# First SwiGLU products: four plain pairs, four pairs by seven products, three plain pairs

## The chip, the core and the metric

The kernel runs on one core of one Trainium2 chip. TensorE (PE) multiplies matrices: a weight load (PEld) puts a 128x128 block into the array, and a matmul streams up to 512 columns past it and adds up in one of eight PSUM banks. VectorE (DVE) and ScalarE (ACT) work elementwise, GpSimd (POOL) does small things and issues transfers, and SyncE (SP) issues most transfers from HBM. The metric is device time in microseconds (us), the median of several runs.

## The reference

Two layers, each a half-step SwiGLU, a mixer and a second half-step SwiGLU, on x of 512 positions by 1024 features in float32; each step adds its result to x and normalizes. The part that matters here is the SwiGLU, which runs four times:

```python
def swiglu(x, w13, w2):
    a, b = jnp.split(x @ w13, 2, axis=-1)
    return (jax.nn.silu(a) * b) @ w2
...
    x = layer_norm(ALPHA * x + 0.5 * swiglu(x, ffn1_w13[l], ffn1_w2[l]), ln_g[l, 0], ln_b[l, 0])
```

`w13` is 1024 x 5632 (2816 for a, 2816 for b), `w2` is 2816 x 1024. "First products" are x @ w13, "second products" the ones with w2.

## The kernel before

Every float32 factor is split into a high part hi (rounded to the matmul type float32r, by ACT) and a rest lo (source minus hi, by DVE); `split` does both. A product is three matmuls: hi by hi, hi by lo, lo by hi.

**First products.** The 2816 hidden features are 22 blocks of 128. For block j, `blocks` fetches 128 columns of w13 for a and 128 for b (`weights`: a transfer of 512 KB into a `raw` tile, then the split into two `w` tiles), and takes two PSUM banks. `pair_of` multiplies them with x (`xh`, `xl`, features on partitions, 512 positions as columns): 8 steps over the 1024 features, 3 matmuls each, for a and for b. `glu` applies Silu on ACT (tile `sa`) and multiplies on DVE into the result tile r of pair k = j % 11: blocks k and k + 11 form a pair. In three of the four SwiGLUs the first two blocks run in halves of 256 positions, since x comes out of the normalization bit by bit (`need`), and their weights lie in other tiles (`early`).

**Second products.** The class `Seven` forms r @ w2 by Strassen's scheme in Winograd's form: per block pair, seven products of half-size blocks in place of eight, whose factors are sums and differences of quarters. `activation_sums(k)` makes the sums of r (DVE, split, and for k of 8 and more a copy to DRAM); `weight_sums(k)` loads 1 MB of w2, makes four sums on DVE and writes them to DRAM through POOL. Both follow each finished pair in `glu`. `run` then goes through the products in order of k, with `mm`, 3 matmuls of 512 columns at a time.

**Order.** The kernel is written for a layer that makes the engines' programs from this text: it sets all waits and gives out tiles by tag, and its queues need not follow the text's order. The tags that matter: `w` (10 tiles of 4 KB per partition, hi and lo of weights in work), `raw` (4, weights as loaded), `h` (33, everything that stays longer: x, r, sums, early weights), `rs` (2, w2 quarters while their sums are made), `sa` (3, half-size work tiles), `ps` (the 8 banks).

Of the kernel before, what the change touches and what calls it, by code (L numbers as in the profile page):

```python
# [24 lines left out]
F32 = mybir.dt.float32  # L28
F32R = mybir.dt.float32r
I32 = mybir.dt.int32  # L30
AF = mybir.ActivationFunctionType
ALU = mybir.AluOpType
AX = mybir.AxisListType

P = 128
D = 1024
T = 512
DEPTH = 2
DFF = 2816
NF = DFF // P  # L40
# [42 lines left out]
def trunk(ctx: ExitStack, tc, x_in, xt_in, w13, w2, w_in, w_br, w_out, ln_g, ln_b, lb_in, hgn, sgg, sgb, sgws,  # L83
          sgbs, masks, tril_in, ident_in, out):
    nc = tc.nc
    V, S, G, PE = nc.vector, nc.scalar, nc.gpsimd, nc.tensor
# [3 lines left out]
    wk = ctx.enter_context(tc.tile_pool(name="wk", bufs=1))  # L90
    psum = ctx.enter_context(tc.tile_pool(name="psum", bufs=8, space=bass.MemoryType.PSUM))

    flow = Flow()
    MM = 216.0

    def bank(name):
        return psum.tile([P, 512], F32, tag="ps", name=name)
# [4 lines left out]
    def slot(name, dtype=F32):  # L102
        return big.tile([P, 2, 512], dtype, tag="h", name=name, bufs=NS)
# [10 lines left out]
    xh, xl = [None] * 4, [None] * 4  # L114


    def split(hi, lo, src):
        S.activation(hi, src, AF.Copy)  # L118
        V.tensor_tensor(lo, src, hi.bitcast(F32), op=ALU.subtract)  # L119

    def weights(src, name, early=False):

        raw = wk.tile([P, D], F32, tag="raw", name=f"r_{name}", bufs=NRAW)
        nc.sync.dma_start(raw, src)
        if early:
            hi, lo = (slot(f"{c}_{name}", F32R).rearrange("p a t -> p (a t)") for c in "hl")
        else:
            hi, lo = (wk.tile([P, D], F32R, tag="w", name=f"{c}_{name}", bufs=NW) for c in "hl")
        split(hi, lo, raw)
        return hi, lo  # L130

    NW = 10
    NS, NRAW, NSA = 33, 4, 3

    def proj(ps, w, c0, mov, nk=KT, n0=0, n=T):

        hi, lo = w
        i = 0
        for k in range(nk):
            cs = slice(c0 + k * P, c0 + (k + 1) * P)  # L140
            mh, ml = mov(k)
            for a, m in ((hi, mh), (hi, ml), (lo, mh)):
                PE.matmul(ps[:, n0:n0 + n], a[:, cs], m[:, n0:n0 + n], start=(i == 0), stop=(i == 3 * nk - 1))  # L143
                i += 1
            flow.tick(3 * MM * n / T)
# [5 lines left out]
    def begin_features():  # L151
        for q in range(4):
            xh[q], xl[q] = slot(f"xh{q}", F32R), slot(f"xl{q}", F32R)
# [26 lines left out]
    H = slice(0, 512), slice(512, 1024)  # L180
# [6 lines left out]
    def norm(t, xt, sums, g, b, last, wait=11500.0):  # L187


        nm = small("nm")  # L190
        V.tensor_scalar(nm, sums[:, 0:1], sums[:, 1:2], -1.0 / D, op0=ALU.add, op1=ALU.mult)
        sq = wk.tile([P, D], F32, tag="rs", name="sq", bufs=2)
        ssq = small("ssq")
        S.activation(sq, xt, AF.Square, bias=nm, accum_out=ssq)
        rstd = rstd_of(ssq, 1, 1.0 / D, LN_EPS / ALPHA ** 2, "rstd")
        for qs in H:
            V.scalar_tensor_tensor(xt[:, qs], xt[:, qs], nm, g[:, qs], op0=ALU.add, op1=ALU.mult)
            V.scalar_tensor_tensor(xt[:, qs], xt[:, qs], rstd, b[:, qs], op0=ALU.mult, op1=ALU.add)
            if last:
                nc.sync.dma_start(out[0, t * P:(t + 1) * P, qs], xt[:, qs])  # L200
        if not last:
            x_at[t] = dram.tile([P, D], F32, name=f"xd{t}", tag=f"xd{t}", bufs=2)
            nc.gpsimd.dma_start(x_at[t], xt)
            ready[t] = flow.add(to_features(t, xt), wait)
# [3 lines left out]
    def need(*ts):  # L208
        for t in ts:
            if ready[t] is not None:  # L210
                flow.finish(ready[t])
                ready[t] = None
# [40 lines left out]
    def quads(name, dtype=F32):  # L253
        return slot(name, dtype).rearrange("p a t -> p (a t)").rearrange("p (q t) -> p q t", q=4)

    NH2 = NF // 2

    class Seven:
# [11 lines left out]

        def part(self, k, a):

            if k not in self.r:
                self.r[k] = quads(f"r{k}")
            return self.r[k][:, a::2, :]

        def weight_sums(self, k):
            w = self.w_of(k)
# [51 lines left out]
        def run(self, c, ln, last):  # L330
# [103 lines left out]
            for tt in range(2):  # L434
# [5 lines left out]
                add_to(xs[t], 0, c, F[tt], sums[t])  # L440
                norm(t, xs[t], sums[t], g, b, last)

    def ffn(l, i, last=False, first_of_all=False):
        made = list(range(Seven.KEPT, NH2)) + list(range(Seven.KEPT))
        seven = Seven(lambda k: w2[l, i, k])
        js = [j for k in made for j in (k, k + NH2)]

        def blocks(j, early=False):
            return (weights(w13[l, i, j], f"a{j}", early), weights(w13[l, i, NF + j], f"b{j}", early),
                    bank(f"pa{j}"), bank(f"pb{j}"))  # L450

        def pair_of(j, args, n0, n):
            wa, wb, pa, pb = args
            proj(pa, wa, 0, from_x, KT, n0, n)
            proj(pb, wb, 0, from_x, KT, n0, n)

        def glu(j, args):
            wa, wb, pa, pb = args
            k, a = j % NH2, j // NH2
            sa = wk.tile([P, T], F32, tag="sa", name="sa", bufs=NSA)  # L460
            S.activation(sa, pa, AF.Silu)
            V.tensor_tensor(seven.part(k, a), sa.rearrange("p (h t) -> p h t", h=2),  # L462
                            pb.rearrange("p (h t) -> p h t", h=2), op=ALU.mult)
            if a:
                seven.activation_sums(k)
                seven.weight_sums(k)

        start = 0 if first_of_all else 2
        first = [blocks(j, True) for j in js[:start]]
        need(0, 1)  # L470
        for z, j in enumerate(js[:start]):
            pair_of(j, first[z], 0, 256)
        need(2, 3)
        for z, j in enumerate(js[:start]):
            pair_of(j, first[z], 256, 256)
            glu(j, first[z])
        for z, j in enumerate(js[start:]):
            if z == 0 and first_of_all:
                begin_features()
                wa = load_wx(w13[l, i, j])  # L480
                for q in range(1, 4):
                    load_xt(q)
                wb = weights(w13[l, i, NF + j], "b0")
                args = wa, wb, bank("pa0"), bank("pb0")
            else:
                args = blocks(j)
            pair_of(j, args, 0, T)
            glu(j, args)
        seven.run(0.5 / ALPHA, (l, 2 * i), last)

    def gates():
# [353 lines left out]
    def load_xt(q):  # L845

        raw = wk.tile([P, D], F32, tag="raw", name=f"xt{q}", bufs=NRAW)
        nc.sync.dma_start(raw, xt_in[q])
        for k in range(2):
            split(xh[q][:, k, :], xl[q][:, k, :], raw[:, k * T:(k + 1) * T])  # L850

    def load_wx(w):

        raw = wk.tile([P, D], F32, tag="raw", name="r_a0", bufs=NRAW)
        hi, lo = (wk.tile([P, D], F32R, tag="w", name=f"{c}_a0", bufs=NW) for c in "hl")
        rx = wk.tile([P, D], F32, tag="raw", name="xt0", bufs=NRAW)
        for z in range(2):
            zs = slice(z * 512, (z + 1) * 512)
            nc.sync.dma_start(raw[:, zs], w[:, zs])
            nc.sync.dma_start(rx[:, zs], xt_in[0, :, zs])  # L860
            split(hi[:, zs], lo[:, zs], raw[:, zs])
            split(xh[0][:, z, :], xl[0][:, z, :], rx[:, zs])
        return hi, lo

    prep = flow.add(prepare(), 30000.0)
    for l in range(DEPTH):
        ffn(l, 0, first_of_all=(l == 0))
        if l == 0:
            flow.finish(prep)
        mixer(l, lb, om)  # L870
        ffn(l, 1, last=(l == DEPTH - 1))
# [98 lines left out]
```

## Time and profile before

| what | us |
| --- | --- |
| median of 3 runs | 2115.67 |
| range of these | 2115.6 to 2118.93 |
| profiled execution, its own time | 2116.28 |
| its span, first to last instruction | 2114.5 |
| first products of the first SwiGLU, first matmul | 5.7 |
| first Silu to last Silu over all four SwiGLUs | 16.4 to 1995.2 |

In the profile a line names the engine, the line of the kernel, the operation, the tile written and the tiles read, the shapes, a count, and then busy time and the mean duration of one in ns; the last field is the time that the engine sat idle before such instructions and what ended it. Timeline rows begin with start and duration in us. Tiles here: `pa`, `pb` the banks of a block, `h_a`, `l_a`, `h_b`, `l_b` its split weights, `r_a`, `r_b` these as loaded, `sa` the Silu, `ra_w`, `rb_w` the quarters of w2.

### The profile page before, as it was taken

The numbers are of one execution on the slowest core, as the hardware profiler recorded it, in microseconds if no ns is written. First come the engines' busy times: TensorE is split into PE (matmuls) and PEld (weight loads), VectorE is DVE, ScalarE is ACT, GpSimd is POOL, SyncE is SP. The second block draws the span as 40 slices with busy tenths as digits, with TensorE's granted clock in tenths as the row PEclk, the third lists the DMA queues.
The fourth block names the chain that finished last, engine by engine and source line by source line (L and its number), as shares of the span: only waits on it lengthen the run. The fifth ranks groups of instructions, "written<-read, shape, count | busy, mean of one in ns | idle before, by whom it ended". The sixth has DMA issues, their size and how long they took to land. (4 is left out here: it accounts for less than half of the span.)

```text
span 2114.5 us, 26531 instructions
## 1 busy us (share of the span) xinstructions
PE 2096.8 (99%) x10024; PEld 1760.8 (83%) x10024; DVE 1226.2 (58%) x2019; ACT 771.4 (36%) x1090; POOL 211.4 (10%) x360
## 2 busy tenths in 40 slices
PE   8999999999999999999999999999999999999998
PEld 6888888888888988888898888888888889888886
DVE  5545578853535745548754456779444456454586
ACT  4222354223422422225522224552343224222363
POOL 0101102001000211101111010020010001110101
PEclk9999999999999999999999999999999999999999
DMA  7665777122242465567756566761222425555674
GB/s 267 216 211 177 247 262 256 44 77 89 81 156 93 176 235 177 195 210 268 248 192 233 178 208 234 270 230 41 90 81 91 143 95 208 205 200 198 223 258 146
DMA packets 113904, 381.01 MB, mean 180 GB/s; under 512 B 14320, under 2 KB 14576, under 8 KB 113776
## 3 DMA queue, kind: packets, MB, share of 16 engines
q1 hardware_dynamic: 88848, 291.68, 42.1%
q0 software_dynamic: 24928, 87.64, 10.9%
q8 instruction: 78, 1.28, 0.3%
q14 instruction: 50, 0.41, 0.1%
HBM read 311.11 MB, written 68.16 MB: 179 GB/s over the span
## 5 line engine op out<-in xcount | busy, mean ns | idle before, releaser
L143 PE MATMUL pa<-xh,h_a 128*128 128x512 f32 (+1 forms) x752 | 284.4, 378 | 6.2 <-ACT xh L118 6.1
L143 PE MATMUL pa<-xl,h_a 128*128 128x512 f32 (+1 forms) x752 | 284.5, 378 | 0.0
L143 PE MATMUL pa<-xh,l_a 128*128 128x512 f32 (+1 forms) x752 | 283.6, 377 | 0.0
L143 PE MATMUL pb<-xh,h_b 128*128 128x512 f32 (+1 forms) x752 | 282.8, 376 | 0.0
L143 PE MATMUL pb<-xh,l_b 128*128 128x512 f32 (+1 forms) x752 | 282.4, 375 | 0.0
L143 PE MATMUL pb<-xl,h_b 128*128 128x512 f32 (+1 forms) x752 | 282.3, 375 | 0.0
L119 DVE TENSOR_TENSOR l_b<-r_b,h_b 128x1024 fp32r<-128x1024 f32 x132 | 161.6, 1225 | 166.8 <-ACT h_b L118 166.3
L118 ACT ACTIVATE h_b<-r_b 128x1024 fp32r<-128x1024 f32 x132 | 140.0, 1061 | 303.6 <-PE pa L143 245.8
L462 DVE TENSOR_TENSOR r<-sa,pb 128x512 f32<-128x512 f32 x88 | 60.6, 688 | 302.0 <-PE pb L143 302.0
L118 ACT ACTIVATE h_a<-r_a 128x1024 fp32r<-128x1024 f32 (+1 forms) x89 | 93.5, 1051 | 274.3 <-PE pb L143 264.7
L143 PEld LDWEIGHTS pa<-xh,h_a 128*128 128x128 f32 x752 | 142.1, 189 | 33.1 <-ACT xh L118 7.4
L143 PEld LDWEIGHTS pa<-xl,h_a 128*128 128x128 f32 x752 | 142.2, 189 | 27.8 <-DVE xl L119 2.0
L143 PEld LDWEIGHTS pa<-xh,l_a 128*128 128x128 f32 x752 | 142.2, 189 | 25.4
L143 PEld LDWEIGHTS pb<-xh,h_b 128*128 128x128 f32 x752 | 141.5, 188 | 25.7
L143 PEld LDWEIGHTS pb<-xl,h_b 128*128 128x128 f32 x752 | 141.5, 188 | 25.6
L143 PEld LDWEIGHTS pb<-xh,l_b 128*128 128x128 f32 x752 | 141.4, 188 | 25.5
L119 DVE TENSOR_TENSOR l_a<-r_a,h_a 128x1024 fp32r<-128x1024 f32 (+1 forms) x89 | 107.8, 1211 | 11.2 <-ACT h_a L118 7.3
L143 PE MATMUL z<-xh,h_z 128*128 128x512 f32 x256 | 102.6, 401 | 0.0
L143 PE MATMUL z<-xh,l_z 128*128 128x512 f32 x256 | 99.8, 390 | 0.0
L143 PE MATMUL z<-xl,h_z 128*128 128x512 f32 x256 | 99.8, 390 | 0.0
L284 POOL DMA_DIRECT2D t<-t x44 | 23.8, 540 | 753.8 <-DVE t L283 687.5
L119 DVE TENSOR_TENSOR l_z<-r_z,h_z 128x1024 fp32r<-128x1024 f32 x32 | 39.2, 1226 | 72.5 <-ACT h_z L118 72.4
(270 smaller groups left out, 4246.3 us busy)
## 6 DMA issues: line engine op xcount, KB each, us to landing
r_b<-in_w_dram SPq DMA_DIRECT2D x88, 512.0 KB, 4.7
r_a<-in_w_dram SPq DMA_DIRECT2D x87, 512.0 KB, 4.8
ra_w<-in_w_dram SPq DMA_DIRECT2D x44, 512.0 KB, 5.4
rb_w<-in_w_dram SPq DMA_DIRECT2D x44, 512.0 KB, 5.0
t<-ra_w POOLq DMA_DIRECT2D x88, 256.0 KB, 2.5
r_c<-in_w_dram SPq DMA_DIRECT2D x44, 512.0 KB, 6.2
r_d<-t SPq DMA_DIRECT2D x44, 512.0 KB, 4.9
r_z<-in_w_in_dram SPq DMA_DIRECT2D x32, 512.0 KB, 3.5
```

Of the source, the lines that this page charges most:

```text
L118: S.activation(hi, src, AF.Copy)
L119: V.tensor_tensor(lo, src, hi.bitcast(F32), op=ALU.subtract)
L143: PE.matmul(ps[:, n0:n0 + n], a[:, cs], m[:, n0:n0 + n], start=(i == 0), stop=(i == 3 * nk - 1))
L284: nc.gpsimd.dma_start(self.t1[k], t1)
L462: V.tensor_tensor(seven.part(k, a), sa.rearrange("p (h t) -> p h t", h=2), pb.rearrange("p (h t) -> p h t", h=2), op=ALU.mult)
```

## The change

The eleven pairs of a SwiGLU are taken in three groups. Pairs 8, 9, 10 and 7 are made as before. Pairs 0 to 3 are made by Strassen's scheme on the first products: x is cut into four quarters (half of the features by half of the positions), the weights of each block into four (half of the features by a or b), and a and b of all positions come from seven products of quarters or of sums of quarters, with A, B, C, E as banks; in a bank the blocks k and k + 11 stand side by side, 256 columns each. Pairs 4, 5 and 6 are again as before.

`x_sums` makes the sums of x once per SwiGLU, after the third block. `weights_of_pair` loads a pair's weights, makes their sums and splits all seven factors: p (two quarters per block as they are), t2 and t13 (sums) into `w` tiles, and c (a quarter as it is) and d (c plus t2) into `h` tiles; for pair 0 it stands ahead of the last block of the first group, and two of its raw quarters are loaded earlier (`raw_cd` with `early`). `seven_pair` runs the products and joins them. Weight sums and activation sums of the second products no longer follow each pair: five weight sums and three activation sums stand in the first group, six and eight in the last.

```diff
@@ -270,9 +271,12 @@
 
         def part(self, k, a):
 
+            return self.room(k)[:, a::2, :]
+
+        def room(self, k):
             if k not in self.r:
                 self.r[k] = quads(f"r{k}")
-            return self.r[k][:, a::2, :]
+            return self.r[k]
 
         def weight_sums(self, k):
             w = self.w_of(k)
@@ -440,13 +444,122 @@
                 add_to(xs[t], 0, c, F[tt], sums[t])
                 norm(t, xs[t], sums[t], g, b, last)
 
+    def x_sums():
+
+        lo_t, hi_t = slice(0, 256), slice(256, 512)
+        r = [slot(f"xr{q}") for q in range(4)]
+        for q in range(4):
+            V.tensor_tensor(r[q], xh[q].bitcast(F32), xl[q].bitcast(F32), op=ALU.add)
+        x3 = quads("xs3")
+        parts = {"s1": [], "s2": [], "s3": [], "s4": []}
+        for q in range(2):
+            a11, a21, a12, a22 = r[q][:, :, lo_t], r[q][:, :, hi_t], r[q + 2][:, :, lo_t], r[q + 2][:, :, hi_t]
+            V.tensor_tensor(x3[:, 2 * q:2 * q + 2], a11, a21, op=ALU.subtract)
+            V.tensor_tensor(a21, a21, a22, op=ALU.subtract)
+            V.tensor_tensor(a22, a11, a21, op=ALU.subtract)
+            V.tensor_tensor(a12, a12, a22, op=ALU.subtract)
+            for c, v in (("s1", a21), ("s2", a22), ("s3", x3[:, 2 * q:2 * q + 2]), ("s4", a12)):
+                parts[c].append(v)
+        s = {}
+        for c in ("s2", "s1", "s3", "s4"):
+            hi, lo = (quads(f"x{c}{v}", F32R) for v in "hl")
+            for q in range(2):
+                split(hi[:, 2 * q:2 * q + 2], lo[:, 2 * q:2 * q + 2], parts[c][q])
+            s[c] = hi, lo
+        return s
+
+    def raw_cd(w13_of, k, early=False):
+
+        if early:
+            rc, rd = slot(f"rc{k}"), slot(f"rd{k}")
+        else:
+            rc, rd = (wk.tile([P, 2, 512], F32, tag="rs", name=f"r{c}{k}", bufs=2) for c in "cd")
+        for z, j in enumerate((k, k + NH2)):
+            nc.sync.dma_start(rd[:, z], w13_of(NF + j)[:, H[0]])
+            nc.sync.dma_start(rc[:, z], w13_of(j)[:, H[1]])
+        return rc, rd
+
+    def weights_of_pair(w13_of, k, rcd=None):
+
+        js = (k, k + NH2)
+        ra = [wk.tile([P, 2, 512], F32, tag="raw", name=f"r_p{j}", bufs=NRAW) for j in js]
+        rc, rd = rcd or raw_cd(w13_of, k)
+        t13 = [slot(f"t13{j}") for j in js]
+        t2 = slot(f"t2{k}")
+        for z, j in enumerate(js):
+            wa, wb = w13_of(j), w13_of(NF + j)
+            nc.sync.dma_start(ra[z][:, 0], wa[:, H[0]])
+            nc.sync.dma_start(ra[z][:, 1], wb[:, H[1]])
+
+        def parts(raw, name, early=False):
+            hi, lo = ((slot(f"{v}_{name}", F32R) if early else
+                       wk.tile([P, 2, 512], F32R, tag="w", name=f"{v}_{name}", bufs=NW)) for v in "hl")
+            split(hi, lo, raw)
+            return [(hi[:, z], lo[:, z]) for z in range(2)]
+
+        p = [parts(ra[z], f"p{j}") for z, j in enumerate(js)]
+        for z in range(2):
+            V.tensor_tensor(t13[z], ra[z], rd[:, z:z + 1].broadcast_to([P, 2, 512]), op=ALU.add)
+            V.tensor_tensor(t2[:, z], ra[z][:, 0], t13[z][:, 1], op=ALU.add)
+        w2 = parts(t2, f"t2{k}")
+        wt = [parts(t13[z], f"t{j}") for z, j in enumerate(js)]
+        w21 = parts(rc, f"c{k}", True)
+        V.tensor_tensor(rc, rc, t2, op=ALU.add)
+        w4 = parts(rc, f"d{k}", True)
+        return p, wt, w2, w21, w4
+
+    def seven_pair(seven, s, k, w):
+
+        p, wt, w2, w21, w4 = w
+        half = slice(0, 256), slice(256, 512)
+        movs = {"A11": lambda m: (xh[m // 2][:, m % 2, half[0]], xl[m // 2][:, m % 2, half[0]]),
+                "A12": lambda m: (xh[2 + m // 2][:, m % 2, half[0]], xl[2 + m // 2][:, m % 2, half[0]]),
+                "A22": lambda m: (xh[2 + m // 2][:, m % 2, half[1]], xl[2 + m // 2][:, m % 2, half[1]])}
+        for c in s:
+            movs[c] = lambda m, c=c: (s[c][0][:, m], s[c][1][:, m])
+
+        def product(ps, units, c, first=True):
+            for z in range(2):
+                hi, lo = units[z]
+                for m in range(4):
+                    ms = slice(m * P, (m + 1) * P)
+                    mh, ml = movs[c](m)
+                    for i, (a, v) in enumerate(((hi, mh), (hi, ml), (lo, mh))):
+                        start = first and z == 0 and m == 0 and i == 0
+                        PE.matmul(ps[:, half[z]], a[:, ms], v, start=start, stop=(m == 3 and i == 2),
+                                  skip_group_check=not (first and z == 0))
+                    flow.tick(3 * 120.0)
+
+        A, B, C, E = (bank(f"f{c}{k}") for c in "ABCE")
+        r = seven.room(k).rearrange("p q t -> p (q t)")
+        lower, upper = r[:, 0:512], r[:, 512:1024]
+        b0, b1 = (wk.tile([P, T], F32, tag="sa", name=f"b{c}", bufs=NSA) for c in "01")
+        product(A, [p[0][0], p[1][0]], "A11")
+        S.activation(upper, A, AF.Copy)
+        product(B, w2, "s2")
+        V.tensor_tensor(upper, upper, B, op=ALU.subtract)
+        product(C, [wt[0][0], wt[1][0]], "s1")
+        V.tensor_tensor(b1, C, upper, op=ALU.subtract)
+        product(E, [wt[0][1], wt[1][1]], "s3")
+        V.tensor_tensor(b1, b1, E, op=ALU.subtract)
+        product(A, w21, "A12", False)
+        S.activation(lower, A, AF.Silu)
+        product(C, [p[0][1], p[1][1]], "s4", False)
+        V.tensor_tensor(b0, C, upper, op=ALU.subtract)
+        V.tensor_tensor(lower, lower, b0, op=ALU.mult)
+        product(E, w4, "A22", False)
+        V.tensor_tensor(upper, E, upper, op=ALU.add)
+        S.activation(upper, upper, AF.Silu)
+        V.tensor_tensor(upper, upper, b1, op=ALU.mult)
+
+    S_PAIRS = 4
+
     def ffn(l, i, last=False, first_of_all=False):
-        made = list(range(Seven.KEPT, NH2)) + list(range(Seven.KEPT))
         seven = Seven(lambda k: w2[l, i, k])
-        js = [j for k in made for j in (k, k + NH2)]
+        w13_of = lambda j: w13[l, i, j]
 
         def blocks(j, early=False):
-            return (weights(w13[l, i, j], f"a{j}", early), weights(w13[l, i, NF + j], f"b{j}", early),
+            return (weights(w13_of(j), f"a{j}", early), weights(w13_of(NF + j), f"b{j}", early),
                     bank(f"pa{j}"), bank(f"pb{j}"))
 
         def pair_of(j, args, n0, n):
@@ -461,31 +574,62 @@
             S.activation(sa, pa, AF.Silu)
             V.tensor_tensor(seven.part(k, a), sa.rearrange("p (h t) -> p h t", h=2),
                             pb.rearrange("p (h t) -> p h t", h=2), op=ALU.mult)
-            if a:
-                seven.activation_sums(k)
-                seven.weight_sums(k)
-
-        start = 0 if first_of_all else 2
-        first = [blocks(j, True) for j in js[:start]]
-        need(0, 1)
-        for z, j in enumerate(js[:start]):
-            pair_of(j, first[z], 0, 256)
-        need(2, 3)
-        for z, j in enumerate(js[:start]):
-            pair_of(j, first[z], 256, 256)
-            glu(j, first[z])
-        for z, j in enumerate(js[start:]):
-            if z == 0 and first_of_all:
-                begin_features()
-                wa = load_wx(w13[l, i, j])
-                for q in range(1, 4):
-                    load_xt(q)
-                wb = weights(w13[l, i, NF + j], "b0")
-                args = wa, wb, bank("pa0"), bank("pb0")
-            else:
-                args = blocks(j)
+
+        front = list(range(Seven.KEPT, NH2)) + [Seven.KEPT - 1]
+        by_seven = list(range(S_PAIRS))
+        behind = list(range(S_PAIRS, Seven.KEPT - 1))
+        sums = iter(range(NH2))
+
+        def plain(j, args=None):
+            args = args or blocks(j)
             pair_of(j, args, 0, T)
             glu(j, args)
+
+
+        js = [j for k in front for j in (k, k + NH2)]
+        if first_of_all:
+            begin_features()
+            wa = load_wx(w13_of(js[0]))
+            for q in range(1, 4):
+                load_xt(q)
+            plain(js[0], (wa, weights(w13_of(NF + js[0]), "b0"), bank("pa0"), bank("pb0")))
+            seven.weight_sums(next(sums))
+            plain(js[1])
+        else:
+            first = [blocks(j, True) for j in js[:2]]
+            need(0, 1)
+            for z, j in enumerate(js[:2]):
+                pair_of(j, first[z], 0, 256)
+            need(2, 3)
+            for z, j in enumerate(js[:2]):
+                pair_of(j, first[z], 256, 256)
+                glu(j, first[z])
+                if z == 0:
+                    seven.weight_sums(next(sums))
+        seven.activation_sums(front[0])
+        seven.weight_sums(next(sums))
+        for z, j in enumerate(js[2:]):
+            args = blocks(j)
+            if z == 5:
+                w = weights_of_pair(w13_of, by_seven[0], rcd)
+            plain(j, args)
+            if z == 0:
+                s = x_sums()
+            if z == 2:
+                rcd = raw_cd(w13_of, by_seven[0], True)
+            if z < 3:
+                seven.weight_sums(next(sums))
+            if z in (1, 3):
+                seven.activation_sums(front[(z + 1) // 2])
+        for k in by_seven:
+            seven_pair(seven, s, k, w if k == by_seven[0] else weights_of_pair(w13_of, k))
+        due = [front[3:] + by_seven[:1], by_seven[1:2], by_seven[2:], behind[:1], behind[1:2], behind[2:]]
+        for z, j in enumerate([j for k in behind for j in (k, k + NH2)]):
+            plain(j)
+            for _ in range((2, 1, 1, 1, 1, 0)[z]):
+                seven.weight_sums(next(sums))
+            for k in due[z]:
+                seven.activation_sums(k)
         seven.run(0.5 / ALPHA, (l, 2 * i), last)
 
     def gates():
```

## Prediction before the change ran

> **What bounds the kernel now.** I read the head of the page first, then the waits of the matmul engine.
>
> ```profile
> span 2114.5 us, 26531 instructions
> PE 2096.8 (99%) x10024; PEld 1760.8 (83%) x10024; DVE 1226.2 (58%) x2019; ACT 771.4 (36%) x1090; POOL 211.4 (10%) x360
> PEclk9999999999999999999999999999999999999999
> PE pa L143 <- ACT xh L118: 6.1, 2, 5.7
> PE pE L340 <- DVE l_d L119: 1.6, 2, 1.0
> ```
>
> PE is busy all along at full clock; the waits recorded for it sum to 7.7 us, 5.7 of it the start. So a change pays what it takes out of PE's stream, as long as the other engines keep that stream fed. A matmul's listed duration is not its cost, because matmuls overlap. What counts is the distance from start to start, from PE's timeline: first three plain blocks (512 columns), then the half-width passes that begin a later SwiGLU (256 columns).
>
> ```profile
> 21.58 0.39 PE L143 MATMUL pa<-xh,h_a 128*128 128x512 f32 x1
> ...
> 54.22 0.39 PE L143 MATMUL pa<-xh,h_a 128*128 128x512 f32 x1
> ```
>
> ```profile
> 1057.03 0.28 PE L143 MATMUL pa<-xh,h_a 128*128 128x256 f32 x1
> ...
> 1062.66 0.28 PE L143 MATMUL pb<-xh,l_b 128*128 128x256 f32 x1
> ```
>
> From 21.58 to 54.22 three blocks of 48 matmuls start: 32.64 / 144 = **226.7 ns** each. From 1057.03 to 1062.66 there are 47 distances: 5.63 / 47 = **119.8 ns**. Half the columns cost 53%, not 50%: about 13 ns of each matmul does not depend on its width. A new weight load belongs to every matmul in both cases, so the half-width row already holds what the new products do: 256 moving columns, a 128x128 load each.
>
> **The matmuls.** A plain pair (blocks k and k + 11, each with its a and b half) is 4 x 8 x 3 = 96 matmuls: 96 x 0.2267 = 21.76 us. The new pair is 7 products x 2 x 4 x 3 = 168 half-width ones: 168 x 0.1198 = 20.13 us, 2.88 us a product. Gain 1.63 us a pair; four pairs in each of four SwiGLUs make 16: **26.1 us**. An eighth of the multiplications goes, but only 7.5% of the time, since 72 more matmuls pay the fixed 13 ns.
>
> [...]
>
> **What the matmuls now need from DVE and ACT.** Durations of the nearest groups, all shapes kept apart:
>
> ```profile
> L119 DVE TENSOR_TENSOR l_b<-r_b,h_b 128x1024 fp32r<-128x1024 f32 x132 | 161.6, 1225 | 166.8 <-ACT h_b L118 166.3
> L462 DVE TENSOR_TENSOR r<-sa,pb 128x512 f32<-128x512 f32 x88 | 60.6, 688 | 302.0 <-PE pb L143 302.0
> L288 DVE TENSOR_TENSOR ra_w<-ra_w 128x512 f32<-128x512 f32 x44 | 30.3, 688 | 0.0
> L119 DVE TENSOR_TENSOR xl<-xt,xh 128x512 fp32r<-128x512 f32 x8 | 5.3, 690 | 3.0 <-ACT xh L118 2.9
> L307 DVE TENSOR_TENSOR s<-r 128x256 f32<-128x256 f32 x44 | 18.7, 426 | 1.5
> L118 ACT ACTIVATE h_b<-r_b 128x1024 fp32r<-128x1024 f32 x132 | 140.0, 1061 | 303.6 <-PE pa L143 245.8 <-PE pb L143 31.2 <-PE pC L340 14.7
> L118 ACT ACTIVATE xh<-xt 128x512 fp32r<-128x512 f32 x8 | 4.7, 624 | 3.5 <-DMA xt<-in_xt_dram 3.4
> L461 ACT ACTIVATE sa<-pa 128x512 f32<-128x512 f32 x88 | 51.0, 579 | 8.1 <-PE pa L143 8.1
> ```
>
> A *plain pair* asks DVE for 4 splits of 1.225 and 2 products of 0.688: 6.3 us in 21.8. A *new pair* asks for 7 splits and 3 adds of the same size (10 x 1.225), 2 half-size adds and 7 half-size outputs (9 x 0.688): 12.25 + 6.19 = **18.4 us in 20.1**. ACT has 7 x 1.061 and four outputs of about 0.58: 9.7 us. `x_sums` adds once per SwiGLU 4 x 1.225 + 8 x 0.688 + 8 x 0.690 = 15.9 us of DVE and 8 x 0.624 = 5.0 of ACT. The broadcast operand of the t13 adds has no row of its own; its bounds are the 1.225 of an equal-sized add and twice that, and I take the first, as it moves the same elements. DVE in sum: 1226 + 4 x 15.9 + 16 x (18.4 - 6.3) = 1483 of about 2090 us. It has room on the mean; the new stage is where it could fail.
>
> So the stage itself. DVE's timeline at the start of the third SwiGLU shows whether preparation waits behind older outputs:
>
> ```profile
> 1060.74 1.21 DVE L119 TENSOR_TENSOR l_a<-r_a,h_a 128x1024 fp32r<-128x1024 f32 x1
> 1061.88 1.22 DVE L119 TENSOR_TENSOR l_b<-r_b,h_b 128x1024 fp32r<-128x1024 f32 x1
> ...
> 1066.33 1.21 DVE L119 TENSOR_TENSOR l_a<-r_a,h_a 128x1024 fp32r<-128x1024 f32 x1
> ...
> 1077.08 0.69 DVE L462 TENSOR_TENSOR r<-sa,pb 128x512 f32<-128x512 f32 x1 [4.88 <-PE pb L143]
> ```
>
> The splits at 1060.74 to 1066.33 belong to the third and fourth block; in the text they stand behind the output of the first, which runs at 1077.08. The queues are thus not in the text's order: ready work goes ahead. I conclude that the next pair's splits run between the present pair's outputs, and that tiles, not text, limit how far ahead. A pair takes all ten `w` tiles: four for p, two for t2, four for t13. Times within a pair: the t2 weights come free at 5.8 (second product), t13's at 11.5 (fourth), p's at 17.3 (sixth). The next pair's p0 can go in at 5.8, p1 and t2 at 11.5, t13 at 17.3, where they are needed at 20.1, 20.1 to 23.0 and 25.9. The shortest cover is thus 8.6 us. What lies in it: two outputs of 0.69, one ACT split of 1.06, two DVE splits of 1.225: 4.9 us. Hidden. With c, their add and d ahead of it too (3 x 1.225) it is 8.6: just covered.
>
> Other waits that the change adds. The banks A, C and E are written a second time: A's reader is a copy on ACT, C's and E's are DVE outputs, each with at least two products (5.8 us) between; behind a late reader PE itself would stand, as its later matmuls queue there. Two pairs' banks fit in the eight. The first pair's weights are asked for ahead of the last plain block: there the `w` tiles come free by halves of a block, the last two at its end, and are needed in the second half of the third product, 7.2 us later, for 2.3 us of split. What is charged here is the entry into the stage, where x sums, glu outputs and 13.6 us of preparation (10 x 1.225 + 2 x 0.688) meet within the last two blocks: between 0 and one late pair of splits (2 x 1.225 = 2.45) per SwiGLU. I take **0.5 us each, 2 us in all**, near the lower end, as DVE was only half busy in a plain stretch:
>
> ```profile
> 1125.60:1300.00 174.40, 174.40 (x771) 144.44 (x771) 87.22 (x128) 50.08 (x65) 18.33 (x34) 1.00 0.59 199
> ```
>
> (columns: length, busy PE, PEld, DVE, ACT, POOL, clock, DMA share, GB/s.)
>
> **What is moved.** Weight sums leave the pairs: five run in the first blocks, none in the new stage, six in the six plain blocks behind it; activation sums of eight pairs also come there. Their DVE time in those 65.3 us: 6 x 4 x 0.688 + 8 x (5 x 0.42 + 0.69) = 38.8, with 6 x 3.14 of the blocks 57.7 us, 88%. Each weight sum loads 1 MB through SP and writes 1 MB through POOL with one pair of `rs` tiles:
>
> ```profile
> rb_w<-in_w_dram SPq DMA_DIRECT2D x44, 512.0 KB, 5.0
> t<-rb_w POOLq DMA_DIRECT2D x44, 256.0 KB, 4.8
> r_b<-t SPq DMA_DIRECT2D x44, 256.0 KB, 4.4
> ```
>
> Load 5.0, four adds 2.75, last write 4.8: 12.6 us round, six of them 75 us, so the last may end some 10 us into the second products. There they are first read in order of k, 4.1 us of PE per k (18 x 0.2267), the last after 41 us: hidden, with about 30 us left. If that cover were gone the price would be those 10 us in each of four SwiGLUs. In the new stage SP issues eight loads of 256 KB (4.4 us each to land) per pair in place of four of 512 KB; the bytes stay 2 MB per 20 us, half of the 199 GB/s above. I cost these at nothing.
>
> **Sum.** The profiled execution took 2116.28, 1.8 over its span and 0.6 over the median of 2115.67. 2116.28 - 26.1 + 2.0 = 2092.2 for that one, **2091.5 us** for the median.
>
> **Rivals.**
> - *DVE is late, a little, in each pair.* For it: 18.4 of 20.1 us, in one queue with outputs that wait for PE. Against: listed durations overlap their neighbours (1060.74 to 1061.88 is 1.14 for a 1.21), so 18.4 is really about 17. If the preparation of c and d goes first and 1.225 more with it, each pair behind another (12 of them) loses about 1 us: 2104.
> - *The other side: tiles go round in a fixed turn.* If the next pair's p tiles are the very ones that the present pair's p leaves, nothing can start before 17.3. Outputs 1.4, p 2.45, t13 2.45, t2 1.4, its split 1.2 follow on DVE: 26.2, needed at 23.0. Each of the 12 pairs behind another loses 3.2 us, 38 in all against 26 gained: 2115.7 + 12.3 = 2128. It decides from 26.1 / 12 = 2.2 us late per pair. For it: no row shows which free tile is taken. Against: t13 and its sums need no `w` tile and could be made earlier, as the early splits above are.
> - *The moved sums are not hidden*: 10 us in each SwiGLU against 26: 2130 at the worst, 2105 where a third shows. Against: 30 us of cover.
> - *The new products run at the load's pace.* The load's own duration speaks for it:
>
> ```profile
> L143 PEld LDWEIGHTS pa<-xh,h_a x752: 186/188/330, 5.7 to 1993.3; 128*128 128x128 f32 x188
> ```
>
> 188 ns a matmul would make a pair 31.6 us: 2115.7 + 16 x 9.8 = 2273. Against: 47 distances of 119.8 with such loads among them, so loads overlap each other too. [...]
>
> **How the numbers follow.** Forecast 0.76; late DVE 0.12; fixed turn 0.06; moved sums 0.05; load pace 0.01. Below the forecast lies little: 2089.6 with no stall at all, and some 0.1% of spread. The range goes from 2087 to 2105, which takes in the forecast, the late DVE and the milder half of the moved sums, about 0.88, and some doubt within the cases brings it to 0.8. A measurement here can tell about 0.2%, 4 us. Faster: 0.76 + 0.12 + about 0.03 = 0.91; slower: fixed turn, load pace and a rest of the sums, 0.07; within 0.2%: 0.02.
>
> **What would show it.** Right: half-width matmuls 120 ns apart throughout the new stage, 20.1 us from one pair's first matmul to the next; PE still 99% busy; no new wait of PE over 2 us. DVE some 17 us busy per pair, at about 85%. Wrong: waits of PE on the l or h tiles of p, t or t2 (the fixed turn, or a late DVE), on an f bank by way of a DVE output, or of pA, pB, pC on l_b or l_t after the plain blocks (the sums).

## The result, and the profile after

| | us |
| --- | --- |
| median before (9 runs) | 2115.67 (2113.89 to 2120.57) |
| median with the change (9 runs) | 2103.18 (2100.62 to 2110.74) |
| ratio | 0.9946, 95% interval 0.9932 to 0.9959 |
| profiled execution of the change | 2110.74, span 2109.0 |

The kernel became faster by 12.5 us, not by the 24 forecast, and its runs now differ by 10 us where they differed by 7. The profiled execution is the slowest of the nine, so its stalls are on the large side. First its page, PE's waits and DVE's waits (line, what it waited for, us in total, times, longest):

```profile
span 2109.0 us, 29248 instructions
PE 2078.6 (99%) x11176; PEld 1796.3 (85%) x11176; DVE 1456.3 (69%) x2307; ACT 838.4 (40%) x1186; POOL 211.5 (10%) x360
```

```profile
PE pa L144 <- ACT xh L119: 5.5, 1, 5.5
PE pA L344 <- DVE l_b L120: 3.7, 5, 1.2
PE fB L529 <- DVE l_t L120: 2.5, 4, 0.8
PE fB L529 <- ACT h_t L119: 2.4, 2, 1.5
PE pA L344 <- ACT h_b L119: 2.0, 3, 1.1
```

```profile
DVE t L287 <- DMA ra_w<-in_w_dram: 95.6, 26, 9.4
...
DVE ra_w L292 <- DMA rb_w<-in_w_dram: 18.8, 16, 2.8
```

PE has new waits in two places: at fB, the second product of the first pair of a new stage (the t2 weights), and at pA, where the second products begin. And DVE has one that the kernel before did not show among its waits: 26 of the 44 weight sums make it stand at their first add (line 287) until the w2 quarters have landed.

The new products themselves run as forecast. PE's timeline of the third SwiGLU, first matmul of the second, third and fourth pair:

```profile
1170.69 0.28 PE L529 MATMUL fA<-xh,h_p 128*128 128x256 f32 x1
...
1190.85 0.28 PE L529 MATMUL fA<-xh,h_p 128*128 128x256 f32 x1
...
1211.01 0.28 PE L529 MATMUL fA<-xh,h_p 128*128 128x256 f32 x1
```

20.16 us from pair to pair (20.13 was forecast), so nothing stops PE between pairs. Where the rest went shows when the profiled executions are cut at the first matmul of each part, read off PE's timelines; each column sums the four SwiGLUs (us). "All first products" includes the new stage; "second products, begin" runs from the first matmul on pA to the first on the c weights, which come next (198 matmuls each).

| kernel | all first products | of it the new stage | second products, begin |
| --- | --- | --- | --- |
| before | 972.8 | - | 179.5 |
| the change | 955.4 | 330.5 | 190.2 |
| v2_more_tiles (below) | 948.5 | 322.5 | 179.5 |

Sixteen pairs at 20.16 are 322.6. The change's stage has 7.9 us more, all of it in the first pair of each SwiGLU, and the begin of the second products takes 10.7 us longer than before. Of the 26.1 us that the matmuls should bring, this execution kept 5.5 (spans 2114.5 and 2109.0). These two places hold 18.6 of the 20.6 us that are missing.

**How the stall comes about.** The end of the first group in the second SwiGLU: SP's, ACT's, DVE's and PE's timelines (start, duration; in brackets the idle time before and what ended it).

```profile
783.05 0.33 SPq L285 DMA_DIRECT2D ra_w<-in_w_dram  x1
```

```profile
781.36 1.06 ACT L119 ACTIVATE h_p<-r_p 128x1024 fp32r<-128x1024 f32 x1 [4.97 <-DMA r_p<-in_w_dram]
```

```profile
776.63 1.22 DVE L120 TENSOR_TENSOR l_p<-r_p,h_p 128x1024 fp32r<-128x1024 f32 x1
787.20 0.69 DVE L287 TENSOR_TENSOR t<-ra_w 128x512 f32<-128x512 f32 x1 [9.36 <-DMA ra_w<-in_w_dram]
787.81 0.68 DVE L575 TENSOR_TENSOR r<-sa,pb 128x512 f32<-128x512 f32 x1
...
792.48 1.22 DVE L120 TENSOR_TENSOR l_p<-r_p,h_p 128x1024 fp32r<-128x1024 f32 x1
...
794.22 1.22 DVE L502 TENSOR_TENSOR t<-r_p,rd 128x1024 f32<-128x1024 f32 x1
...
800.21 1.22 DVE L120 TENSOR_TENSOR l_t<-t,h_t 128x1024 fp32r<-128x1024 f32 x1
```

```profile
798.40 0.28 PE L529 MATMUL fA<-xh,l_p 128*128 128x256 f32 x1
800.18 0.39 PE L529 MATMUL fB<-xs2h,h_t 128*128 128x256 f32 x1 [1.50 <-ACT h_t L119]
...
801.49 0.38 PE L529 MATMUL fB<-xs2h,l_t 128*128 128x256 f32 x1 [0.81 <-DVE l_t L120]
```

The fifth weight sum's load starts at 783.05, since its tile was still being written out for the fourth. It lands at 787.2, and for 9.36 us DVE does nothing, with a Silu product, a split of p, the t13 adds and the split of t2 queued behind the add. That split of p could have run at 782.4, when ACT had made its high part, but it ran at 792.48: on DVE what stood behind the waiting add waited too. The work then runs off one piece after another, and when PE is through with the first product, at about 798.5, t2 is not there: PE stands 1.50 us for its high part and 0.81 for the rest. What held the load is in SP's own waits, first before, then with the change:

```profile
SPq L281 <- DMA t<-ra_w: 68.7, 40, 9.2
```

```profile
SPq L285 <- DMA t<-ra_w: 180.1, 35, 10.1
```

Before as well as after, most of the 44 loads of ra_w waited for the transfer that carries the previous sum out of the same `rs` tile, but before for 1.7 us on the mean and now for 5.1. Before the change there was one sum per pair, every 21.8 us. In the last group there is now one per block of 10.9 us, and with two `rs` tiles the loads follow each other only every 11.4 to 12.2 us (second to sixth load of the group, mean of each SwiGLU).

### The profile page after: what moved, and what is told of

It is laid out like the page before. It is cut to its first block, busy times and chain, and to the rows that moved or that the text cites. A ratio compares the mean times of both kernels' runs of the same rounds, so it can differ in the third digit from the quotient of the medians.

```text
span 2109.0 us, 29248 instructions
## 1 busy us (share of the span) xinstructions
PE 2078.6 (99%) x11176; PEld 1796.3 (85%) x11176; DVE 1456.3 (69%) x2307; ACT 838.4 (40%) x1186; POOL 211.5 (10%) x360
## 5 line engine op out<-in xcount | busy, mean ns | idle before, releaser
L144 PE MATMUL pa<-xh,h_a 128*128 128x512 f32 (+1 forms) x496 | 184.4, 372 | 5.6 <-ACT xh L119 5.5
L144 PE MATMUL pa<-xl,h_a 128*128 128x512 f32 (+1 forms) x496 | 184.6, 372 | 0.7 <-DVE xl L120 0.6
L144 PE MATMUL pa<-xh,l_a 128*128 128x512 f32 (+1 forms) x496 | 183.5, 370 | 0.0
L144 PE MATMUL pb<-xh,l_b 128*128 128x512 f32 (+1 forms) x496 | 182.9, 369 | 0.5 <-DVE l_b L120 0.5
L144 PE MATMUL pb<-xh,h_b 128*128 128x512 f32 (+1 forms) x496 | 183.2, 370 | 0.0
L144 PE MATMUL pb<-xl,h_b 128*128 128x512 f32 (+1 forms) x496 | 182.7, 368 | 0.0
L144 PEld LDWEIGHTS pa<-xh,h_a 128*128 128x128 f32 x496 | 93.9, 189 | 22.2 <-ACT xh L119 6.5
L144 PEld LDWEIGHTS pa<-xl,h_a 128*128 128x128 f32 x496 | 93.9, 189 | 18.8 <-DVE xl L120 3.3
L144 PEld LDWEIGHTS pa<-xh,l_a 128*128 128x128 f32 x496 | 94.0, 189 | 15.4
L144 PEld LDWEIGHTS pb<-xl,h_b 128*128 128x128 f32 x496 | 93.5, 188 | 15.7
L287 DVE TENSOR_TENSOR t<-ra_w 128x512 f32<-128x512 f32 x44 | 30.4, 690 | 95.9 <-DMA ra_w<-in_w_dram 95.6
```

Of the source, the lines that this page charges most:

```text
L287: V.tensor_tensor(t1, a[:, 0], a[:, 1], op=ALU.add)
```

## The experiments

Three theories. **S**: a weight sum's load comes late because its two `rs` tiles are still busy, DVE's queue stands at the first add, and what stands behind it reaches PE late. **D**: DVE simply has too much to do at the entry to the new stage and behind it. **T**: the w2 transfers crowd out the loads of the first weights. The kernel before was timed again beside the experiments, and the ratios go by these times: 2114.68 us for the first four runs below, 2115.92 for the other four.

### Sums left out, quarters copied

```diff
-            a, b = (wk.tile([P, 2, 512], F32, tag="rs", name=f"r{c}_w2{k}", bufs=2) for c in "ab")
...
-                V.tensor_tensor(dst, u, v, op=ALU.add)
-                nc.gpsimd.dma_start(to, dst)
+            nc.gpsimd.dma_start(self.t1[k], w[:, 0])
+            nc.gpsimd.dma_start(self.t34[k][:, 0], w[:, 1])
+            nc.gpsimd.dma_start(self.t2[k // 2][:, k % 2], w[:, 2])
+            nc.gpsimd.dma_start(self.t34[k][:, 1], w[:, 3])
```

> The changed kernel, but the weight sums of the second products are left out: the four quarters of w2 are copied from HBM to HBM into the places of the sums (as many bytes read and written, by POOL's transfers). No add of these on DVE, no rs tile. Theory S (the weight sums' loads come late, DVE's queue stands at their first add, and splits and outputs behind it come late to PE): the waits of PE on t2 and on l_b, h_b are gone, 2091 us (2089 to 2094). Rival D (DVE simply has too much to do at the entry to the new stage and behind it): only 2.75 us of each sum goes, about half of the loss stays, 2097. Rival T (the transfers themselves crowd out the loads of the first weights): 2103, as before the edit.

Measured: 2105.19 us, ratio 0.9954 (0.9939 to 0.9969). On its face this is T's number, but the parts look different. In the second to fourth SwiGLU every new stage takes 80.63 us and every begin of the second products 44.88, no stall at all. The whole loss is in the first: its first group takes 99.2 us (91.6 in the change) and its stage 88.9. The reason is an effect of the edit that I had not foreseen: with no tile to wait for, the copies of all four SwiGLUs start at once, and the last of them has landed at 208.9 us. The DMA share in tenths over 40 slices:

```profile
DMA  9999387223243433237733234771222434323374
```

The first four slices, 210 us, are at 9, a share of 90% or more. So such crowding cost time in this group: 99.2 us against 91.6. The three other SwiGLUs lose nothing, but they have neither the sums' waits nor the adds nor the transfers any more, so each of the three theories would free them. The run settles nothing between them.

### Sums on POOL

The four adds go to POOL: `V.tensor_tensor` in `weight_sums` becomes `G.tensor_tensor`.

> The changed kernel with the four adds of each weight sum on POOL in place of DVE; loads, tiles and writes stay. S: POOL stands at the loads, DVE does not; 2091 to 2096, as far as POOL's adds (no row shows one of this size) keep up. D: about 2097, since DVE has 121 us less to do. T: 2103.

Measured: 2171.32 us, ratio 1.0268 (1.0253 to 1.0283): slower, a miss for all three. POOL's groups (mean ns, idle before) and PE's longest wait:

```profile
L287 POOL TENSOR_TENSOR t<-ra_w 128x512 f32<-128x512 f32 x44 | 76.6, 1741 | 517.6 <-DVE r L549 355.5 <-DMA ra_w<-in_w_dram 113.8 <-DVE s L311 18.7
L292 POOL TENSOR_TENSOR rb_w<-rb_w,ra_w 128x512 f32<-128x512 f32 x44 | 65.2, 1481 | 0.9
```

```profile
PE pB L344 <- DVE l_t L120: 32.2, 4, 11.4
```

An add takes 1.35 to 1.74 us on POOL against 0.69 on DVE, so each round grows by some 3 us, and the sums end so late that the second products wait for t2 itself (11.4 us once). The run says nothing between S and D; it shows that a longer round of the sums makes the kernel slower.

### The new order with plain products

```diff
-        for k in by_seven:
-            seven_pair(seven, s, k, w if k == by_seven[0] else weights_of_pair(w13_of, k))
+        for j in [j for k in by_seven for j in (k, k + NH2)]:
+            plain(j)
```

(x sums, `raw_cd` and the first pair's preparation go too.)

> The order of the change without its products: pairs 0 to 3 are plain, x sums and the seven products are left out, the weight and activation sums stand where the change puts them. S: DVE waits for w2 loads show in front and behind, and the wait of the second products' start (7 to 11 us in the profiled run of the change) comes back: 2120 to 2126, slower than before the change. D: DVE has little to do, so 2116, as before the change. T: 2120 to 2126.

Measured: 2126.77 us, ratio 1.0055 (1.0040 to 1.0070), just above what S and T had. The moved sums alone make the kernel before *slower* by 12 us. By the spans the profiled executions differ by 9.5 us, and the begin of the second products alone takes 10.1 more: 189.6 us for 179.5. DVE's and PE's waits:

```profile
DVE t L287 <- DMA ra_w<-in_w_dram: 109.8, 31, 6.9
```

```profile
PE pA L344 <- DVE l_b L120: 2.8, 4, 0.8
PE pA L344 <- ACT h_b L119: 2.5, 2, 1.6
```

No seven products, no x sums, and still the same waits. D had 2116 here, since it took DVE to have little to do; but the six blocks of the last group ask DVE for the same work as in the change, so D is weakened and not yet out. S and T stand.

### More tiles for the sums

```diff
-            a, b = (wk.tile([P, 2, 512], F32, tag="rs", name=f"r{c}_w2{k}", bufs=2) for c in "ab")
+            a, b = ((slot(f"r{c}_w2{k}") if k % 2 else wk.tile([P, 2, 512], F32, tag="rs", name=f"r{c}_w2{k}", bufs=2))
+                    for c in "ab")
```

> The changed kernel with the tiles of every second weight sum out of the h tiles, so that one sum's load need not wait for the last one's writes; every instruction stays. S: the 96 us that DVE waits for w2 loads fall below 20, PE's waits on t2 and l_b shrink to 1 or 2 us in all, 2092 us (2090 to 2096). D: 2103, DVE's work is the same. T: 2103 or more, since the same bytes come in a shorter time.

Measured: **2090.43 us** (2089.07 to 2091.09), ratio to before 0.9882 (0.9866 to 0.9899): better than both kernels. PE, DVE, ACT and POOL run as many instructions as in the change, and as many bytes are moved; only tiles were added. DVE's waits for the sums' loads, then PE's waits:

```profile
DVE t L288 <- DMA ra_w<-in_w_dram: 17.0, 9, 3.1
...
DVE ra_w L293 <- DMA rb_w<-in_w_dram: 0.3, 1, 0.3
```

```profile
PE pa L144 <- ACT xh L119: 6.1, 2, 5.4
PE pa L144 <- DVE xl L120: 0.7, 1, 0.7
PE pE L345 <- DVE l_d L120: 0.6, 1, 0.6
PE pb L144 <- DVE l_b L120: 0.5, 1, 0.5
```

Neither fB nor pA is among PE's waits any more; every new stage takes 80.63 us, every begin of the second products 44.88. D would have kept its loss, as DVE's work is the same; T would have kept or raised it, as the same bytes come in less time. The last group of the second SwiGLU shows both, first in the change, then here (length, busy PE, PEld, DVE, ACT, POOL, clock, DMA share, GB/s):

```profile
879.10:944.41 65.31, 65.31 (x291) 54.06 (x289) 42.93 (x74) 19.47 (x30) 10.79 (x20) 1.00 0.70 235
870.65:935.96 65.31, 65.31 (x290) 54.08 (x289) 48.54 (x86) 22.00 (x33) 12.98 (x24) 1.00 0.79 273
```

In the same 65.31 us DVE now does 5.6 us more and the transfers move more, and nothing is late behind it. S holds: the shortage of tiles is the cause. One thing stays open. The layer that makes the engines' programs also ordered the queues anew: in this SwiGLU the first add of the fifth sum stood behind a split of p in the change (787.20), and stands ahead of splits of the last two plain blocks here (758.83). How much each of the two does, a load that comes earlier and an add that stands elsewhere, no run tells apart.

### One group at a time

The same edit with `k % 2 and k < 5` (first group) and with `k % 2 and k >= 5` (last group).

> More tiles as in the run before, but only for weight sums of the first group of pairs (1 and 3); the last group has its two rs tiles as in the change. If both groups' sums cost on their own: the new stage runs at 80.6 us in all four SwiGLUs, the start of the second products stays longer than its 44.9 us (45 to 52), 2094 to 2101. If only the first group's sums matter and the rest follows from them: 2091.

> The other half: more tiles only for weight sums 5, 7 and 9 in the last group. If both groups' sums cost on their own: the new stage stays at 81 to 84 us, the start of the second products is back at 44.9, 2093 to 2099. If the last group's waits follow from the first group's: 2103, unchanged.

Measured: front alone 2097.79 us (ratio 0.9915, 0.9899 to 0.9931), behind alone 2094.78 (0.9901, 0.9886 to 0.9915). With tiles in front the new stages are at 80.63 and the begin of the second products still at up to 49.95; with tiles behind the begin is at 44.88 in all four and the stages at 81.0 to 82.0. Each group costs on its own: 5.4 us for the first, 8.4 for the last, 13.8 in sum where both together gave 12.7. The first of these is the less certain, as the runs with tiles in front lie between 2094.6 and 2101.0.

### Plain products, new order, more tiles

> All pairs plain in the order of the change (x sums and seven products left out), with more tiles for every second weight sum. S: the order costs nothing once no sum waits for its tiles, 2114 to 2116, as before the change. D and T: 2120 or more, since the order still crowds DVE and the transfers.

Measured: 2116.81 us, ratio 1.0002 (0.9993 to 1.0011). The order is free once the sums have tiles: the 12 us of the plain run above are gone.

### Five pairs

```diff
-    S_PAIRS = 4
+    S_PAIRS = 5
...
-            if z < 3:
+            if z < 4:
                 seven.weight_sums(next(sums))
```

(On the tiles of v2; the two plain pairs left get `due` of 3, 2, 2, 1 activation sums and 2, 1, 1, 1 weight sums.)

> More tiles, and five pairs by seven products in place of four; six weight sums in the first group, five in the last, whose two pairs get all eight activation sums. If matmuls alone set the time again: 4 x 1.63 = 6.5 us less than with four, 2084. If DVE is next: the last group asks DVE for 4 x 3.14 + 5 x 2.75 + 8 x 2.79 = 48.7 us in 43.5 us of PE, so up to 5 us late in each SwiGLU, 2086 to 2104.

Measured: 2103.24 us, ratio 0.9940 (0.9924 to 0.9957): 12.8 slower than with four. The stage is at 100.79 us in three of four SwiGLUs, 5 x 20.16, so the products pay again; but PE waits once more where the second products begin (47 to 52 us each):

```profile
PE pA L345 <- DVE l_b L120: 10.5, 4, 4.2
```

The forecast had DVE's 48.7 us in the last group not fit into 43.5. The trace shows DVE late but not full: in the last group of the second SwiGLU it is busy for 35.0 of 43.55 us, and the rest of its work runs on into the second products.

```profile
896.22:939.77 43.55, 43.55 (x194) 36.06 (x193) 34.98 (x67) 15.66 (x25) 8.21 (x16) 1.00 0.80 266
```

DVE also waits for sums' loads again (29.9 us in all), so the run does not show whether its work or these waits make it late.

## Why the prediction was right and wrong

- **The matmuls: right.** 20.16 us a pair against 20.13; v2 as a whole is 24 to 25 us faster than the kernel before, of the 26.1 that were worked out for 16 pairs.
- **DVE in the new stage: right.** All second to fourth pairs follow without a stop, v2 by 20.16 us throughout. DVE's busy time in the first two pairs of the second SwiGLU there (length, busy PE, PEld, DVE, ACT, POOL, clock, DMA share, GB/s):

```profile
790.02:810.18 20.16, 20.16 (x170) 20.16 (x169) 17.36 (x19) 9.45 (x10) 0.00 (x0) 1.00 0.32 105
810.18:830.34 20.16, 20.16 (x171) 20.16 (x170) 17.14 (x20) 9.03 (x10) 0.00 (x0) 1.00 0.34 106
```

  17.3 us of 20.16, as the rival's "really about 17" had it. The t13 adds with a broadcast operand took the lower bound, 1.22 us. The late DVE and the fixed turn of tiles did not come about, nor the load's pace.
- **The failed step: "What is moved", where the weight sums are costed at nothing.** I worked out the round of a sum, 12.6 us, saw that six of them take longer than the six blocks beside them, and then asked only who needs the sums, and when: not before the second products, 30 us of cover. That was so: in the change no load of a finished sum waited for its writing. What I left out is what is queued *behind* the waiting add: DVE's splits and outputs for PE. A round longer than a block (11.4 to 12.2 us measured, against 10.9) means that the loads fall behind the blocks, and each add is a place where DVE can stop. The rival "the moved sums are not hidden" had the place behind and a mechanism of late sums, at 0.05; the mechanism was DVE's queue, and it struck in front as well. Measured cost at the median: 2103.18 - 2090.43 = 12.7 us, where the sum had 0 for this.
- **The entry at 2 us: mis-sized, as part of the same thing.** With tiles in front alone 5.4 us come back. The 2.45 us per SwiGLU that I gave as the upper end is not a bound, since it allowed for late splits but not for a DVE that stands still: in the profiled execution the first two new stages took 3.7 and 2.8 us more than 80.63.
- **The signs.** Two of those given for "wrong" came: waits on the t2 tiles and waits of pA on l_b. The prediction read them as a fixed turn of tiles or a late DVE, and as late sums; here both had one other cause. One sign for "right" could not tell: PE is 99% busy before and after.
- **What was luck.** The measured 2103.18 lies inside the range, beside the 2104 of "DVE is late" and the 2105 of "a third" of the moved sums, but neither mechanism is what happened. With the one cause removed the time is 2090.4, 1.1 us from the forecast; that it is so near is luck in part, since the forecast held 2 us for the entry of which v2 shows nothing, and v2's first products are shorter by 24.3 us, not by 26.1.

## What to carry to other kernels

Work that is off the critical path still stands in an engine's queue, and here a split of p that was ready at 782.4 ran at 792.48, behind a waiting add: when such work is moved, ask not only when its result is needed but what is queued behind its wait. Compare the round of its buffers (load, work, write out) with the pace at which it is issued; here it was longer (11.4 to 12.2 us against 10.9), the loads fell behind, and the wait ended in the shared engine (95.6 us of DVE's idle time at the first adds). A second set of buffers (here two more tiles for every second sum, out of a larger pool) can be worth as much as the algorithm: 12.7 us beside the 12.5 that the change had brought.

## What the hardware showed besides

Two stalls of PE were followed by a stretch at half clock, which cost time on top of them. In the change's second SwiGLU PE stands 1.14 and 0.76 us for the second products' weights, and then runs at half clock. PE's timeline and the windows (columns as above):

```profile
968.93 0.50 PE L344 MATMUL pA<-h_b,th 128*128 128x512 f32 x1 [1.14 <-ACT h_b L119]
970.20 0.64 PE L344 MATMUL pA<-l_b,th 128*128 128x512 f32 x1 [0.76 <-DVE l_b L120]
970.63 0.63 PE L344 MATMUL pA<-h_b,tl 128*128 128x512 f32 x1
```

```profile
967.00:970.40 3.40, 1.50 (x6) 0.73 (x5) 1.49 (x2) 2.58 (x4) 0.00 (x0) 1.00 0.95 361
970.40:973.80 3.40, 3.40 (x9) 2.62 (x9) 2.99 (x4) 3.40 (x6) 0.00 (x0) 0.50 0.68 188
973.80:977.00 3.20, 3.20 (x16) 2.62 (x15) 3.20 (x6) 3.20 (x6) 0.00 (x0) 1.00 0.68 200
```

For 3.4 us the granted clock is 0.50 and matmuls start 0.43 us apart, not 0.227: nine of them cost 1.7 us more, nearly as much as the stops. An earlier half clock, in the new stage of the first SwiGLU, runs from 103.42 to 106.83, behind stops of 0.87 and 0.80 us for the t2 weights (first matmuls after them at 100.97 and 102.27); the half-width matmuls start 0.21 us apart there, not 0.12. The stops of 1.50 and 0.81 us at 798.7 to 801.5 were longer in sum than either pair, and no half clock followed: the first two windows below, and the next 3.42 us too, are at 1.00. The third is the one ahead of the earlier half clock.

```profile
796.32:799.74 3.42, 2.36 (x20) 2.16 (x18) 3.38 (x4) 0.67 (x1) 0.00 (x0) 1.00 0.99 362
799.74:803.15 3.41, 2.16 (x16) 1.96 (x17) 3.41 (x4) 3.21 (x4) 0.00 (x0) 1.00 0.65 231
100.00:103.42 3.42, 1.75 (x12) 1.45 (x12) 3.42 (x4) 3.22 (x4) 0.00 (x0) 1.00 0.83 288
```

PE is busy for 2.36 and 2.16 us in the windows of the stall that half clock did not follow, and for 1.50 and 1.75 us in the ones just ahead of half clock. What decides between the two, no run here shows.
